# The first norm's scales as diagonal matrices, matmuls on ones ahead of it, and another order of the first loads

## The chip, the cores and the metric

The kernel runs on one core of one Trainium2 chip. The metric is device microseconds of one execution; the kernel before was run three times (median 1280.13 us). A core has five engines with an in-order queue each: TensorE (PE, its weight loads shown apart as PEld), VectorE (DVE), ScalarE (ACT), GpSimd (POOL) and SyncE (SP), which here issues every DMA. Engines wait for each other by semaphores; a waiting instruction holds up all that stands behind it on its engine.

## The reference

One decoder layer on 1024 tokens of 1024 channels, in float32:

```python
h = rms_norm(x, norm_pre_mix)          # x * rsqrt(mean(x*x) + eps) * g, row by row
p = h @ w_in                           # 1024 x 2720: conv columns, r, k, v, and low-rank wd, ad, gd
...                                    # token shift, RWKV-7 recurrence over 8 heads of 64,
decay = f(tanh(wd) @ decay_up)         # the two low-rank products that the change speaks of
a = sigmoid(iclr_a0 + ad @ iclr_up)
g = sigmoid(gd) @ gate_up
...                                    # causal convolution (31 taps), layer norm, silu
x = x + rms_norm(concat(rwkv, conv) @ w_out, norm_post_mix)
f = conv_ffn(rms_norm(x, norm_pre_ffn))   # 1024 -> 2 x 2816 -> 1024, 3-tap convolution, gelu gate
out = x + rms_norm(f, norm_post_ffn)
```

The change touches only the first norm, the projection's beginning and the loading of the low-rank weights.

## The kernel before

**Precision.** PE multiplies float32 operands at full speed only in a rounded form. Every product is therefore made of three matmuls: both operands are split into a high part (a rounded copy) and a low part (the difference), and hi x hi, hi x lo and lo x hi are summed. For a weight, `weight` (L164) loads it into `wr` (three buffers), ACT casts it to `wh` and POOL subtracts to get `wl` (both at L162, two buffers each). In the first half of the tokens SP also stores each `wl` to DRAM (`lows`, L183), for the second half to read it back (L179); a `wl` buffer can be written again only when PE has read it and its store has landed.

**Order.** The kernel is written with a tile framework. Work belongs to streams with priorities (`PRIO`), `first` ahead of all others; the framework's scheduler merges the streams by priority and its own estimate of times into one fixed order for each engine. `tc.issue_after(i)` keeps what stands under it behind instruction `i` in that order.

**The beginning.** The tokens are taken in halves of 512. For the first half, four row tiles `l` (128 tokens by 1024 channels, as two pieces of 256 KB each) are loaded (`load_rows`, L287) and normed in two pairs (`norm_rows`, L293). For row tiles 0 and 2 ACT sums the squares (L308); for 1 and 3 DVE does it by statistics (L301). DVE forms mean + eps (L156), POOL takes the reciprocal root (L157), ACT scales one piece of the row (L311) and DVE the other (L312). Then `channels` (L258) turns the pair: PE transposes sixteen 128x128 blocks against an identity (L150) into PSUM banks `pe` and `pb`, ACT writes the high part of `h`, scaled by the channel's gain (L277), and DVE the low part (L279). `h` has eight tiles of 128 channels, each with a high and a low part.

Then PE projects. The first weight pair belongs to k0; it is used in two halves of 256 columns, so that the first pair of row tiles suffices to begin (`project` with `halves`, 48 matmuls of 256 columns). The first and second weight of this text are the two halves of k0's first block of 128 outputs, the third and fourth those of its second block (24 matmuls of 512 columns on 128 outputs each), the fifth and sixth are `w_wa`, the columns `wd` and `ad` (64 outputs). After these come k1, r0, r1, and the chunked recurrence of the first quarter.

**Beside it.** The second half's rows (`mixr`, `ck`, `co`) are loaded and normed early, behind the last `h` of the first half. The low-rank weights (`lora`, `lw`) are loaded in `setup_mixer` (L233 to L240): three loads, two casts on ACT, two subtractions on POOL.

The FFN's first norm (`norm_ffn`, L874) does not scale its rows: it multiplies the identity by the root (a diagonal matrix), and PE multiplies the row by that diagonal, which transposes and scales in one matmul. `channels` takes these matrices as `diags`.

## Time and profile before

| | before |
|---|---|
| runs | 1280.13 us median (1280.02 to 1281.09) |
| profiled execution | 1282.25 us, its span 1280.5 us |
| granted TensorE clock, mean | 0.988 |
| busy share of the span | PE 96%, PEld 78%, DVE 70%, ACT 57%, POOL 39% |
| DMA | 185.70 MB, mean 145 GB/s |

A row of a timeline reads: start, duration, engine, source line, operation, output tile <- input tiles, shape, number of instructions merged, and in brackets how long the engine had been idle before it and what ended that. A row of a group reads: instructions merged, then busy us and mean ns of one, then idle us before them and what ended most of it. `SPq` rows are issues of DMAs by SP, not the transfers.

### The profile page before, as it was taken

Reading aid. Unit: us, or ns where it says so; the run is one execution under the profiler, and the core shown is the slowest. Engines: PE = TensorE matmul, PEld = TensorE weight load, DVE = VectorE, ACT = ScalarE, POOL = GpSimd, SP = SyncE. Lnnn points to the kernel's source line nnn. Section 1 sums busy time; section 2 is a strip of 40 time slices with the busy share of each in tenths; the row PEclk is TensorE's granted clock in tenths of the full one; section 3 lists DMA queues with packets and bytes.
Section 4 is the critical chain, followed back from the end, with each engine's and each line's share of the span. In section 5 each row is a group of like instructions: output and inputs, shape, how many; then the busy total and the mean of one; then the engine's idle time right before and its main releaser. Section 6 shows DMA issues by size and latency. Waiting matters only on the chain.

```text
span 1280.5 us, 23025 instructions
## 1 busy us (share of the span) xinstructions
PE 1231.8 (96%) x8460; PEld 993.7 (78%) x8460; DVE 892.2 (70%) x1540; ACT 731.3 (57%) x1518; POOL 495.6 (39%) x438
## 2 busy tenths in 40 slices
PE   6989989999999989999999999999999999999997
PEld 5767767787778867788789878787778888888885
DVE  5286998997679989996621275655366678479568
ACT  6563564655844865656743277777455566444451
POOL 4343320011113332344455269897688860000001
PEclk9999999999999999999999999999999999999999
DMA  7544442343342461222345498887423245335523
GB/s 241 171 137 138 118 127 76 107 133 116 109 131 89 133 192 44 84 79 80 108 137 159 133 335 304 287 310 238 157 67 82 71 159 190 91 114 187 162 73 132
DMA packets 105505, 185.70 MB, mean 145 GB/s; under 512 B 15184, under 2 KB 21712, under 8 KB 105392
## 3 DMA queue, kind: packets, MB, share of 16 engines
q1 hardware_dynamic: 105392, 184.23, 45.5%
q8 instruction: 67, 1.10, 0.4%
q14 instruction: 46, 0.38, 0.1%
HBM read 141.58 MB, written 42.60 MB: 144 GB/s over the span
## 4 chain that ended last, share of the span: by engine, by line
PE 58%; DVE 8%; issue 2%; POOL 2%; DMA 2%; ACT 2%; SPq 0%; POOLq 0%; DVEq 0%; ACTq 0%
PE pb L135 27%; PE pe L135 13%; PE xs L135 12%; PE Y L135 2%; PE pc L135 2%; DVE pc L416 2%; DVE nrow L1116 1%; POOL wl L162 1%; DVE x L1100 1%; PE pc L150 1%; DMA pt<-mixd 1%; DMA m<-mixd 1%; POOL b L1056 1%; PE pe L150 0%; DVE m L162 0%
## 5 line engine op out<-in xcount | busy, mean ns | idle before, releaser
L162 POOL TENSOR_TENSOR wl<-wr,wh 128x512 fp32r<-128x512 f32 (+1 forms) x181 | 237.5, 1314 | 251.0 <-ACT wh L162 219.8
L162 ACT CAST wh<-wr 128x512 fp32r<-128x512 f32 (+1 forms) x220 | 135.4, 616 | 174.4 <-issue 46.1
L135 PE MATMUL pb<-h,wh 128*128 128x512 f32 (+3 forms) x720 | 228.8, 397 | 3.2 <-ACT wh L162 1.6
L135 PE MATMUL pb<-f,wh 128*128 128x512 f32 x696 | 221.9, 399 | 2.5 <-ACT wh L162 1.5
L416 DVE SCALAR_TENSOR_TENSOR pc<-c,params,pc 128x512 f32<-128x512 f32 x232 | 174.3, 751 | 8.7 <-ACT pc L413 4.7
L135 PEld LDWEIGHTS pb<-h,wh 128*128 128x128 f32 (+2 forms) x720 | 131.2, 188 | 36.0 <-ACT wh L162 3.7
L135 PEld LDWEIGHTS pb<-f,wh 128*128 128x128 f32 x696 | 130.9, 190 | 32.4 <-ACT wh L162 2.8
L135 PE MATMUL pb<-h,wl 128*128 128x512 f32 (+3 forms) x360 | 146.1, 406 | 2.1 <-POOL wl L162 2.0
L135 PE MATMUL pb<-f,wl 128*128 128x512 f32 x348 | 139.0, 400 | 0.9 <-POOL wl L162 0.9
L157 POOL TENSOR_TENSOR ss<-var,mhalf 128x1 f32<-128x1 f32 x16 | 11.0, 692 | 226.9 <-DVE ss L1097 202.8
L1056 POOL TENSOR_TENSOR b<-b,b 128x512 f32<-128x512 f32 x66 | 86.9, 1319 | 2.6 <-DMA b<-ffn_down 1.0
L135 PE MATMUL pe<-f,wh 128*128 128x512 f32 x272 | 85.4, 395 | 0.1
L135 PEld LDWEIGHTS pb<-h,wl 128*128 128x128 f32 (+2 forms) x360 | 67.3, 187 | 20.1 <-POOL wl L162 4.1
L135 PEld LDWEIGHTS pb<-f,wl 128*128 128x128 f32 x348 | 66.3, 190 | 16.7 <-POOL wl L162 2.0
L135 PE MATMUL xs<-f,wh 128*128 128x512 f32 x200 | 62.7, 395 | 0.4 <-DVE act L953 0.4
L135 PEld LDWEIGHTS pe<-f,wh 128*128 128x128 f32 x272 | 51.0, 188 | 11.7 <-ACT wh L162 0.3
L899 DVE SCALAR_TENSOR_TENSOR pt<-pb,params,pt 128x511 f32<-128x511 f32 (+1 forms) x48 | 35.7, 744 | 31.6 <-ACT ecarry L892 31.1
L162 POOL TENSOR_TENSOR wl<-b,wh 128x512 fp32r<-128x512 f32 x36 | 47.0, 1305 | 22.4 <-ACT wh L162 20.7
L135 PE MATMUL pe<-f,wl 128*128 128x512 f32 x136 | 53.8, 396 | 0.7 <-POOL wl L162 0.7
L706 POOL TENSOR_TENSOR XG<-r,GE 64x256 f32<-64x256 f32 x30 | 20.4, 683 | 87.1 <-DVE r L725 82.3
L178 ACT CAST wh<-wr 128x512 fp32r<-128x512 f32 (+2 forms) x44 | 26.5, 604 | 43.5 <-PE pb L135 31.2
L162 ACT CAST wh<-b 128x512 fp32r<-128x512 f32 x36 | 22.2, 617 | 47.4 <-PE pb L135 19.2
(428 smaller groups left out, 2896.8 us busy)
## 6 DMA issues: line engine op xcount, KB each, us to landing
wr<-ffn_up SPq DMA_DIRECT2D x117, 256.0 KB, 2.8
wr<-w_in SPq DMA_DIRECT2D x80, 256.0 KB, 3.0
b<-ffn_down SPq DMA_DIRECT2D x44, 256.0 KB, 4.4
sums<-b SPq DMA_DIRECT2D x44, 256.0 KB, 3.9
wr<-sums SPq DMA_DIRECT2D x44, 256.0 KB, 2.7
lows<-wl SPq DMA_DIRECT2D x40, 256.0 KB, 3.3
wl<-lows SPq DMA_DIRECT2D x40, 256.0 KB, 2.6
b<-ffn_up SPq DMA_DIRECT2D x40, 256.0 KB, 2.7
```

The costliest lines, as they stand in the source:

```text
L135: return self.nc.tensor.matmul(out, lhsT, rhs, start=start, stop=stop, skip_group_check=skip)
L150: self.nc.tensor.transpose(out, in_, self.con("ident")[:n, :n])
L157: self.nc.gpsimd.tensor_tensor(out, v[:, :n], self.mhalf[:, :n], ALU.pow)
L162: return self.nc.scalar.copy(hi, src), eng.tensor_tensor(lo, src, hi.bitcast(F32), ALU.subtract)
L178: self.nc.scalar.copy(hi, raw)
L416: nc.vector.scalar_tensor_tensor(out, c[:, j:j + HALF], w(j), acc, ALU.mult, ALU.add)
L706: nc.gpsimd.tensor_tensor(x[64:128], R[64:128, gs], w.GE[64:128, c, gs].unsqueeze(2).broadcast_to([64, 4, CH]), ALU.mult)
L899: nc.vector.scalar_tensor_tensor(acc[:, o:], ps[:, :HALF - o], w(j), acc[:, o:], ALU.mult, ALU.add)
L1056: sub = lambda o, x, y, op=ALU.subtract: self.nc.gpsimd.tensor_tensor(o, x, y, op)
L1100: nc.vector.scalar_tensor_tensor(x, f[c], s[:, 1:2], x, ALU.mult, ALU.add)
L1116: nc.vector.tensor_tensor(out, a, b, op)
```

## The change

1. **Diagonals.** `norm_rows` takes `dg`; for the first half's rows it no longer scales, but writes a 128x128 diagonal for each row tile into one `pt` tile. `channels` then multiplies by these. The second pair uses the PSUM banks `pc`, `xs` (two) and `Y`, which have no other use yet, instead of `pe` and `pb`.
2. **Ones.** POOL fills a tile with ones, and PE multiplies it by itself seven times (`WARM`) into bank `pc`, before anything else. The result is not used.
3. **Order of the first loads.** Now: identity, row tiles 0 and 1, parameters, the first two weights, row tiles 2 and 3, the other constants.
4. **Low-rank weights later.** Their three loads and four operations move from `setup_mixer` to `lora_in`, behind the load and the subtraction of the sixth weight in the scheduler's order, with `t2` tiles for the raw form.
5. **The second half's rows** are loaded behind the issue of the third weight's load.

```diff
+WARM = 7
...
             if self.loaded:
                 raw = self.loaded.pop(0)
+            else:
+                raw = (self.f2p.tile(...) if held is self.hp else self.wp.tile(shape, F32, tag="wr", bufs=3, ...))
+                self.load = self.nc.sync.dma_start(raw, src)
+                self.loads.append(self.load)
...
+        with self.stream("first"):
+            warm = self.tl("co", [P, 512])
+            nc.gpsimd.memset(warm, 1.0)
+            ps = self.bank("pc")
+            for _ in range(WARM):
+                self.mm(ps, warm[:, :P], warm)
+            nc.sync.dma_start(self.const[:, :P], a["consts"][:, :P])
+            two = [self.tl("l8", [P, 2, D]) for _ in range(2)]
+            self.rows = [(two[t // 2][:, t % 2, :512], two[t // 2][:, t % 2, 512:]) for t in range(4)]
+            self.load_rows(0, self.rows[:2])
+            nc.sync.dma_start(self.params, a["params"])
+            for j in range(2):
+                raw = self.wp.tile([P, 4, P], F32, tag="wr", bufs=3, name=self.nm("wr"))
+                self.load = nc.sync.dma_start(raw, a["w_in"][4, j])
+                self.loaded.append(raw)
+            self.load_rows(0, self.rows[2:], 2)
+            nc.sync.dma_start(self.const[:, P:], a["consts"][:, P:])
...
+    def lora_in(self):
+        nc, a = self.nc, self.a
+        for e in range(2):
+            raw = self.tl("t2", [P, D_RWKV])
+            nc.sync.dma_start(raw, a["lora"][:, e])
+            nc.scalar.copy(self.lw[:, e], raw[0:96])
+            low = self.lw[64:96, e]
+            nc.gpsimd.tensor_tensor(low, raw[64:96], low.bitcast(F32), ALU.subtract)
+        nc.sync.dma_start(self.lora, a["lora"][:G_LORA, 2])
...
             self.rstd(ss[:, 3:4], ss[:, 2:3], 1.0 if t % 2 else 1.0 / D, RMS_EPS)
-            nc.scalar.activation(row[0], row[0], AF.Copy, scale=ss[:, 3:4])
-            nc.vector.tensor_scalar(row[1], row[1], ss[:, 3:4], None, ALU.mult)
+            if dg is not None:
+                nc.vector.tensor_scalar(dg[:, t], self.con("ident"), ss[:, 3:4], None, ALU.mult)
+            else:
+                nc.scalar.activation(row[0], row[0], AF.Copy, scale=ss[:, 3:4])
+                nc.vector.tensor_scalar(row[1], row[1], ss[:, 3:4], None, ALU.mult)
...
+            dg = self.tl("pt", [P, 4, P])
             for b in range(2):
-                two = rows[2 * b:2 * b + 2]
-                self.norm_rows(two)
-                self.channels(two, "pre_mix", hs, slice(b * QUARTER, (b + 1) * QUARTER), ("pe", "pb", "pb"))
+                two = self.rows[2 * b:2 * b + 2]
+                self.norm_rows(two, dg[:, 2 * b:2 * b + 2])
+                self.channels(two, "pre_mix", hs, slice(b * QUARTER, (b + 1) * QUARTER),
+                              ("pc", *self.xs, self.Y) if b else ("pb", "pe"), [dg[:, 2 * b + t] for t in range(2)])
...
-        project(0, hs, "k0 w k1 r0 r1")
+        project(0, hs, "k0 w")
+        behind = self.loads[0], self.load, self.low
+        project(0, hs, "k1 r0 r1")
...
-            self.load_rows(1, rows)
+            with tc.issue_after(behind[0].ins):
+                self.load_rows(1, rows)
+            with tc.issue_after(behind[1].ins), tc.issue_after(behind[2].ins):
+                self.lora_in()
```

The scheduler lays all engines anew from this. Three places of its order follow. The first is POOL at the beginning, where `ss<-var` is the reciprocal root of a row tile, `wl<-wr` the low part of a weight and `lw` that of a low-rank weight. Before:

```order
L157 TENSOR_TENSOR ss_220<-var_226,mhalf 128x1
L240 TENSOR_TENSOR lw<-wr_106,lw 32x512
L240 TENSOR_TENSOR lw<-wr_110,lw 32x512
L162 TENSOR_TENSOR wl_274<-wr_271,wh_273 128x512
L162 TENSOR_TENSOR wl_281<-wr_278,wh_280 128x512
L157 TENSOR_TENSOR ss_689<-var_695,mhalf 128x1
L157 TENSOR_TENSOR ss_700<-var_706,mhalf 128x1
L157 TENSOR_TENSOR ss_711<-var_717,mhalf 128x1
L157 TENSOR_TENSOR ss_722<-var_728,mhalf 128x1
L162 TENSOR_TENSOR wl_340<-wr_337,wh_339 128x512
```

and with the change, from the first half's first root on:

```order
L161 TENSOR_TENSOR ss_157<-var_163,mhalf 128x1
L166 TENSOR_TENSOR wl_271<-wr_114,wh_270 128x512
L161 TENSOR_TENSOR ss_167<-var_173,mhalf 128x1
L166 TENSOR_TENSOR wl_276<-wr_116,wh_275 128x512
L161 TENSOR_TENSOR ss_213<-var_219,mhalf 128x1
L161 TENSOR_TENSOR ss_223<-var_229,mhalf 128x1
L161 TENSOR_TENSOR ss_693<-var_699,mhalf 128x1
L166 TENSOR_TENSOR wl_335<-wr_332,wh_334 128x512
L161 TENSOR_TENSOR ss_704<-var_710,mhalf 128x1
L166 TENSOR_TENSOR wl_354<-wr_351,wh_353 128x512
```

The first two weights' low parts now stand among the first half's roots, and the third's and fourth's (`wl_335`, `wl_354`) among the second half's, where before all of these came ahead of the third (`wl_340`).

The second place is SP from the store of the first low part on. Before:

```order
L183 DMA lows<-wl_274 128x512
L170 DMA wr_379<-w_wa 128x256
L183 DMA lows<-wl_281 128x512
L170 DMA wr_398<-w_wa 128x256
L183 DMA lows<-wl_340 128x512
L170 DMA wr_423<-w_in 128x512
L183 DMA lows<-wl_359 128x512
```

and with the change:

```order
L191 DMA lows<-wl_271 128x512
L191 DMA lows<-wl_276 128x512
L825 DMA po_4713<-post_mix 128x256
L177 DMA wr_393<-w_wa 128x256
L277 DMA t_114_684<-lora 128x512
L277 DMA t_115_688<-lora 128x512
L281 DMA lora<-lora 96x512
L177 DMA wr_418<-w_in 128x512
L191 DMA lows<-wl_335 128x512
L191 DMA lows<-wl_354 128x512
```

The store of the third low part (`wl_340`, now `wl_335`) stood right behind the load of the sixth weight; now three low-rank loads and a seventh weight's load stand between.

The third place is PE at about half of the mixer's first part, where a projection (`pb<-h`) and the recurrence's last step (`xs<-r`, `Y<-r`) meet. Before, nine matmuls of that projection stand ahead of the recurrence, the last of them and the first two of the recurrence being:

```order
L135 MATMUL pb_1890<-h_139,wh_1893 128x512
L135 MATMUL pb_1890<-h_140,wh_1893 128x512
L135 MATMUL pb_1890<-h_139,wl_1894 128x512
L135 MATMUL xs_97<-r_267,ck_1108 64x64
L135 MATMUL Y<-r_267,ca_1041 64x64
```

and with the change:

```order
L139 MATMUL pb_1894<-h_140,wh_1897 128x512
L139 MATMUL pb_1894<-h_141,wh_1897 128x512
L139 MATMUL xs_94<-r_266,ck_1112 64x64
L139 MATMUL Y<-r_266,ca_1045 64x64
```

Two of the nine are left ahead, and seven come behind. From here to the end of the mixer such small shifts run through all engines' orders; behind the mixer the orders are the same.

## The prediction

> **What bounds the kernel now.** I read the page first: which engine is full, and in which part of the span it is not.

> ```profile
> span 1280.5 us, 23025 instructions
> PE 1231.8 (96%) x8460; PEld 993.7 (78%) x8460; DVE 892.2 (70%) x1540; ACT 731.3 (57%) x1518; POOL 495.6 (39%) x438
> ```

> TensorE (PE) is busy for 96% of the span, so a gain has to come out of 48.7 us of PE idle time or out of slow matmuls. The table of windows says where the idle time lies (the columns are window, length, busy time and count for PE, PEld, DVE, ACT, POOL, then granted clock, DMA share, GB/s).

> ```profile
> 0.00:20.00 20.00, 8.48 (x32) 5.97 (x32) 11.04 (x36) 13.56 (x31) 6.82 (x14) 1.00 0.91 305
> 20.00:60.00 40.00, 39.27 (x184) 31.20 (x185) 14.70 (x39) 22.73 (x45) 18.16 (x17) 1.00 0.54 165
> 60.00:640.00 580.00, 556.80 (x5358) 444.23 (x5357) 487.55 (x871) 352.56 (x731) 166.05 (x166) 0.98 0.37 111
> ```

> The change works on the first of them: 11.5 us idle, nearly a quarter of the total. From 20 to 60 us PE misses only 0.7 us, so a lead won at 20 us is kept as far as every feeder of PE keeps pace, and a lead that a feeder does not follow turns into a stall. So I looked next at the timeline of PE over the first projection (k0's first block, 48 matmuls of 256 columns) and the start of the two behind it.

> ```profile
> 8.46 0.48 PE L150 MATMUL pe<-const,l 128*128 128x128 f32 x1 [8.46 <-ACT l L311]
> 20.37 0.77 PE L135 MATMUL pb<-h,wh 128*128 128x256 f32 x2 [0.48 <-DVE h L279]
> 20.93 0.41 PE L135 MATMUL pb<-h,wl 128*128 128x256 f32 x1
> 21.14 0.63 PE L135 MATMUL pb<-h,wh 128*128 128x256 f32 x2
> 27.96 0.28 PE L135 MATMUL pb<-h,wl 128*128 128x256 f32 x1
> 28.08 0.63 PE L135 MATMUL pb<-h,wh 128*128 128x512 f32 x2
> 28.84 0.50 PE L135 MATMUL pb<-h,wl 128*128 128x512 f32 x1
> 34.42 0.39 PE L135 MATMUL pb<-h,wl 128*64 128x512 f32 x1
> ```

> At 21 us matmuls of one size start 0.21 us apart (20.93 to 21.14); at 28 us, 0.12 apart (27.96 to 28.08). PE begins this projection at half rate, although the clock column of the first window reads 1.00. That block ends at 28.08; the third weight's low part is first read at 28.84, the fifth weight's (`w_wa`) at 34.42. These two times are my gauges.

> **The change on PE alone.** A scaled row was two passes (L311 0.72 us, L312 0.48); a diagonal is one small one, and the sixteen transposes of each pair of row tiles become sixteen true matmuls.

> ```profile
> L311 ACT ACTIVATE l<-l,ss 128x512 f32<-128x512 f32 x4 | 2.9, 723 | 1.9 <-POOL ss L157 1.9
> L312 DVE TENSOR_SCALAR l<-l,ss 128x512 f32<-128x512 f32 x4 | 1.9, 476 | 0.0
> 488.92 0.28 DVE L874 TENSOR_SCALAR kk<-const,sf 128x128 f32<-128x128 f32 x1
> 496.17 1.05 PE L135 MATMUL pb<-kk,row 128*128 128x128 f32 x8
> 39.48 1.02 PE L135 MATMUL pe<-kk,const 128*128 128x512 f32 x2
> ```

> The FFN's first norm already does it so: 0.28 us a diagonal, and 8 records in 1.05 us are 4 matmuls of two records, about 0.22 us each at full rate, twice that at half. ACT is rid of 2.9 us, DVE of 1.9 - 4 x 0.28 = 0.8. Seven matmuls on ones are fourteen records; two last some 0.9 us at full rate (1.02 with the last one's tail), so the seven take 6 us, or 12 at half rate, and begin near 1.3 us. They are hidden behind the row loads either way: the second diagonal is not ready before 11.9 us (below). Without that cover they would cost up to 12 us.

> The last diagonal stands at 15.0 to 15.5 us (next part). Fourteen diagonal matmuls behind it (3.1 us) and 48 x 0.12 = 5.8 us of k0 end at 23.9 to 24.4: **PE alone would be 3.7 to 4.2 us ahead** of 28.08.

> Whether the ones keep the rate up until then, the rows leave open: PE has little between the first diagonal (an estimate: 9.4, behind five small operations on the parameters) and the second. If all sixteen to thirty-two diagonal matmuls ran at half rate, k0 would end near 27. I price this at nothing, since the next part is as late; without that cover it is 2.5 us.

> **What PE then waits for: the third weight's low part.** Here the order of the queues counts, and each is in order.

> ```profile
> l<-x SPq DMA_DIRECT2D x8, 256.0 KB, 5.4
> params<-params SPq DMA_DIRECT2D x1, 185.0 KB, 6.5
> 8.00:11.00 3.00, 1.32 (x4) 0.58 (x4) 2.57 (x8) 2.51 (x6) 0.55 (x1) 1.00 1.05 373
> 7.96 0.69 DVE L301 BATCH_NORM_STATS2 bs<-l 128x6 f32<-128x512 f32 x1 [1.01 <-DMA l<-x]
> 9.67 0.55 POOL L157 TENSOR_TENSOR ss<-var,mhalf 128x1 f32<-128x1 f32 x1 [2.02 <-DVE var L156]
> 9.95 0.69 DVE L301 BATCH_NORM_STATS2 bs<-l 128x6 f32<-128x512 f32 x1 [0.36 <-DMA l<-x]
> 9.27 0.63 ACT L308 ACTIVATE pt<-l 128x512 f32<-128x512 f32 x1
> L162 ACT CAST wh<-wr 128x512 fp32r<-128x512 f32 (+1 forms) x220 | 135.4, 616 | 174.4 <-issue 46.1
> ```

> Loads: SP now issues the parameters (185 KB) and the first two weights (512 KB) ahead of row tiles 2 and 3. The seventh of the eight row pieces landed at 9.95, so the eighth, at 373 GB/s, near 10.65. It now has 697 KB more ahead of it: 1.9 us at that rate, 2.3 at the 305 GB/s of the first window. It lands at **12.5 to 13.0**.

> Norm: from a piece's arrival to its root is 9.67 + 0.55 - 7.96 = 2.26 us, and 0.28 for the diagonal: 15.0 to 15.5. On POOL the second root now stands behind the first weight's subtraction. That weight ends 1465 KB of loads (four row pieces, 185, 256), where before the sixth row piece ended 1536 KB and was squared at 9.27: there by 9.2, cast 0.6, subtraction 1.3, root 0.55, diagonal 0.28: 11.9. The second weight's subtraction follows, through by 13, before the last root's input at 14.

> ```profile
> 17.78 1.66 DVE L279 SCALAR_TENSOR_TENSOR h<-pe,params,h 128x256 fp32r<-128x256 f32 x4 [0.36 <-ACT h L277]
> 20.92 0.87 DVE L279 SCALAR_TENSOR_TENSOR h<-pe,params,h 128x256 fp32r<-128x256 f32 x2
> 21.70 1.28 DVE L301 BATCH_NORM_STATS2 bs<-mixr 128x6 f32<-128x512 f32 x2
> 22.90 1.27 DVE L301 BATCH_NORM_STATS2 bs<-co 128x6 f32<-128x512 f32 x2
> 24.52 2.59 POOL L157 TENSOR_TENSOR ss<-var,mhalf 128x1 f32<-128x1 f32 x4 [0.67 <-DVE ss L309]
> 27.47 1.31 POOL L162 TENSOR_TENSOR wl<-wr,wh 128x512 fp32r<-128x512 f32 x1 [0.36 <-ACT wh L162]
> ```

> All sixteen low parts of h now stand on DVE behind the last diagonal: 16 x 1.66/4 = 6.6 us, so 21.6 to 22.1. Before they ended at 20.92 + 0.87 = 21.8: DVE has won nothing. Behind them come the second half's statistics, whose first root ended at 24.52 + 0.65, 3.3 us after 21.8: now 24.9 to 25.4. And POOL now holds the third weight's subtraction behind that root, where before all four roots were long done: + 1.3 us, 26.2 to 26.7, against 28.8. **2.3 us are left of PE's lead at the first gauge**; PE waits near 25 us for about 1.5 to 2.

> **And then for the fifth: a store that SP holds back.**

> ```profile
> 28.81 0.33 SPq L170 DMA_DIRECT2D wr<-w_wa  x1
> 29.19 0.42 SPq L183 DMA_DIRECT2D lows<-wl  x1
> 33.14 0.74 POOL L162 TENSOR_TENSOR wl<-wr,wh 128x256 fp32r<-128x256 f32 x1 [2.63 <-DMA lows<-wl]
> ```

> `wl` has two buffers, so the fifth low part may be written only when the third has been stored to DRAM: 29.19 to 33.14, 3.95 us, and POOL sat idle 2.63 for it. Before, that store stood right behind the second `w_wa` load. Now SP has three low-rank loads (704 KB by their shapes) and the next `w_in` load between, and that last one needs the fourth weight's buffer, which POOL frees after one more root and subtraction: 0.65 + 1.3 = 1.95 us after 26.2 to 26.7. Its own issue takes 0.4 more: store at 28.6 to 29.1, back by 32.5 to 33.0, subtraction (0.74) done by 33.3 to 33.8, against a read at 34.42: **0.6 to 1.1 us of lead at the second gauge.** Bounds: the 704 KB are 1.9 us of transfer at 373 GB/s; if all of them are still queued, the lead turns into a loss of 1 us; if the store lands 0.8 us faster, it is 1.8. I take 0.6, the low end, since by 28.6 most of the 704 KB, issued from 26.5 on, have moved, but not all. Preparing the low-rank weights itself (two casts, two subtractions of 1.25 us) falls where POOL waits for the store, and its user comes after 55 us: nothing.

> Sum: 1282.25 us for the profiled execution - 0.6 = 1281.6; that execution stands 2.1 above the median of the runs, so against 1280.13 I say **1279.5**.

> **Rivals.** (A) *The lead holds.* If the store is back in time, 2.3 us stay; if the two weights do not delay the rows either, PE's 4 us. Middle: 3.1, so 1277.0. For it: 20 to 60 us leaves PE no other wait. Against: the 2.63 us wait on that very store.

> (B) *New gaps bring the half rate back, and the kernel gets slower.* The place is the two waits made above, near 25 and 32 us.

> ```profile
> 388.32 1.62 PE L150 MATMUL pe<-const,l 128*128 128x128 f32 x8 [2.15 <-DVE mixr L760]
> 389.00:392.00 3.00, 3.00 (x14) 2.78 (x13) 3.00 (x8) 2.87 (x6) 0.00 (x0) 0.50 0.20 76
> 392.00:393.00 1.00, 1.00 (x5) 0.53 (x4) 1.00 (x4) 1.00 (x3) 0.00 (x0) 0.93 0.00 0
> ```

> After a gap of 2.15 us the granted clock was 0.50 for 3.4 us: 1.7 us lost. One such stretch gives 1281.2, two or a third in the middle 1282.9; it decides from the second on, as PE is full behind it. [...]

> (C) *The middle is re-laid.* The scheduler's order differs on all engines from about 165 us to the end of the mixer, and is the same from there on.

> ```profile
> 180.00:190.00 10.00, 6.92 (x120) 5.12 (x120) 9.87 (x17) 9.23 (x20) 1.44 (x3) 0.87 0.29 100
> 190.00:200.00 10.00, 9.27 (x34) 7.17 (x34) 9.89 (x16) 3.73 (x6) 0.00 (x0) 0.62 0.00 0
> ```

> Here PE loses 1.3 + 3.8 us to the clock and 3.8 idle. Seven matmuls of a projection now come behind the recurrence and could fill it: up to 3.5 us, 1276.5. Against: DVE is full there and sets the pace.

> (D) *The ones do not do what they are for* (half rate at 16 us): by the price above the time stays the forecast's, so it is no case of its own.

> **Chances.** Forecast 0.40 (its own range 1278.3 to 1280.8), A 0.22, B one stretch 0.10, B two 0.12, C 0.16. Differences under 0.2% (2.6 us) can hardly be told from none. A and C lie mostly below 1277.6: 0.35 faster. B with two lies above 1282.7: 0.13 slower. The rest, 0.52, within. The range for eight times in ten runs from 1276.0, inside A's and C's better ends, to 1282.4, short of B's second stretch.

> **What would show it.** Right: the third weight's subtraction on POOL behind a root, ending near 26.5; PE gaps near 25 and 32 us; POOL idle on the store of `wl` before the fifth; first read of the fifth weight's low part within 1 us of 34.4. The start: 256-column matmuls 0.12 apart from the first if the ones work, 0.21 if not. Wrong: a fifth low part read before 32.5 (A), a clock of 0.50 between 25 and 40 us (B), or a lead that changes by more than 2 us between 160 and 640 us (C).

## The result and the profile after

| | before | changed |
|---|---|---|
| runs taken together | 1281.63 us median of 6 (1280.02 to 1286.07) | 1289.60 us median of 6 (1286.40 to 1292.94) |
| ratio | 1 | 1.0060, 95% interval 1.0037 to 1.0082 |
| profiled execution | 1282.25 us | 1286.4 us, its span 1284.6 us |

The kernel became slower by 0.6%, 8.0 us between the medians. I had forecast 1279.5 with a range up to 1282.4. A second set of six runs of the changed kernel gave 1289.61 (1.0066, 1.0044 to 1.0088). The runs of this text come in six sets; the kernel before was run again in each, and its medians lie between 1281.5 and 1282.8 us. A difference between medians of two sets can be off by as much; the ratios compare within a set.

The page after, its first lines, and the table of windows with the cuts of before (the last window is longer by the difference of the spans):

```profile
span 1284.6 us, 23107 instructions
PE 1241.2 (97%) x8506; PEld 996.9 (78%) x8506; DVE 894.8 (70%) x1540; ACT 729.0 (57%) x1515; POOL 494.9 (39%) x439
```

```profile
0.00:20.00 20.00, 17.31 (x91) 12.39 (x92) 11.67 (x37) 12.08 (x29) 5.97 (x14) 1.00 0.91 318
20.00:60.00 40.00, 36.64 (x173) 28.15 (x172) 15.97 (x38) 22.13 (x44) 19.26 (x18) 1.00 0.52 158
60.00:640.00 580.00, 558.75 (x5358) 444.76 (x5356) 488.50 (x866) 350.73 (x728) 163.19 (x165) 0.98 0.38 111
```

PE is busy for 8.8 us more in the first 20 us (8.5 of it are the ones), for 2.6 us less from 20 to 60, for 2.0 us more from 60 to 640. The share of busy time rose, and the kernel is slower: busy time alone says nothing here.

PE's timeline at the places that the prediction timed, in the changed kernel:

```profile
1.32 8.48 PE L139 MATMUL pc<-co 128*128 128x512 f32 x14 [1.32 <-POOL mhalf L209]
12.06 0.94 PE L139 MATMUL pb<-pt,l 128*128 128x128 f32 x6 [1.37 <-DVE pt L338]
18.39 0.48 PE L139 MATMUL pb<-h,wh 128*128 128x256 f32 x2
18.71 0.28 PE L139 MATMUL pb<-h,wl 128*128 128x256 f32 x1
18.83 0.40 PE L139 MATMUL pb<-h,wh 128*128 128x256 f32 x2
24.22 0.63 PE L139 MATMUL pb<-h,wh 128*128 128x512 f32 x2
26.09 0.50 PE L139 MATMUL pb<-h,wl 128*128 128x512 f32 x1 [1.24 <-POOL wl L166]
33.53 0.45 PE L139 MATMUL pb<-h,wl 128*64 128x512 f32 x1 [1.69 <-POOL wl L166]
```

In this execution the start went as forecast. The ones end at 9.8 us (one matmul on them, float32 as it is and two records, takes 0.86 us at the full clock of 5.8 to 9.6 us; one on the rounded parts, with the same 512 columns, 0.23 at 26.4 to 26.9); matmuls of 256 columns are 0.12 us apart from the first (18.71 to 18.83); k0's first block ends at 24.22 (forecast 23.9 to 24.4, before 28.08). The third low part is read at 26.09 (26.2 to 26.7, before 28.84), the fifth at 33.53 (33.3 to 33.8, before 34.42). What holds the fifth back is what the prediction named. SP's issues and POOL's work there:

```profile
26.44 0.91 SPq L277 DMA_DIRECT2D t<-lora  x2
27.39 0.43 SPq L281 DMA_DIRECT2D lora<-lora  x1
28.41 0.90 SPq L191 DMA_DIRECT2D lows<-wl  x2
```

```profile
24.78 1.26 POOL L166 TENSOR_TENSOR wl<-wr,wh 128x512 fp32r<-128x512 f32 x1
32.76 1.42 POOL L166 TENSOR_TENSOR wl<-wr,wh 128x256 fp32r<-128x256 f32 x2 [3.52 <-DMA lows<-wl]
```

The third low part is done at 26.04, its store is issued at 28.41, behind the low-rank loads, and POOL is idle for 3.52 us until it has landed. So at 34 us the changed kernel was 0.9 us ahead, and at the end 4 us behind, one execution against one. It lost 5 us in a part of the program whose instructions the change does not touch.

To see where, I took the same matmuls of PE in every trace (those at 38, 145, 268, 505, 700 and 1270 us in the kernel before; the first is one of the last of `w_wa`) and the time from one to the next. The number in brackets is an estimate of what granted clock of 0.50 cost there: half of the time at 0.50, since matmuls of 512 columns start 0.43 us apart at 0.50 and 0.23 at 1.00 (the changed kernel's first trace, 74.3 to 79.8 us).

| trace | at | 38-145 | 145-268 | 268-505 | 505-700 | 700-1270 |
|---|---|---|---|---|---|---|
| before | 38.1 | 106.9 (0) | 123.0 (5.1) | 237.0 (5.1) | 195.0 (3.4) | 570.0 |
| changed, first trace | 37.3 | 108.5 (1.7) | 124.5 (6.8) | 238.1 (5.1) | 194.1 (0) | 571.8 |
| changed, second trace | 39.7 | 107.8 (1.7) | 124.6 (6.8) | 238.9 (3.4) | 195.7 (1.7) | 570.2 |
| new start, old middle | 38.4 | 107.5 (1.7) | 122.8 (5.1) | 237.9 (5.1) | 191.9 (0) | 572.9 |
| old start, new middle | 39.8 | 107.7 (0) | 125.0 (6.8) | 241.1 (5.1) | 194.1 (0) | 571.1 |
| first piece new | 38.5 | 107.8 (0) | 124.7 (6.8) | 235.9 (1.7) | 191.9 (0) | 572.8 |
| middle piece new | 37.8 | 107.0 (1.7) | 124.0 (6.8) | 241.6 (5.1) | 191.6 (0) | 573.3 |
| first and middle piece new | 37.9 | 108.3 (1.7) | 124.5 (6.8) | 238.4 (5.1) | 191.6 (0) | 570.0 |
| first piece and end new | 39.8 | 107.9 (0) | 124.8 (6.8) | 235.8 (1.7) | 196.1 (1.7) | 573.3 |
| eight ones | 36.3 | 107.0 (0) | 129.3 (6.8) | 243.3 (3.4) | 192.6 (1.7) | 572.2 |
| ten ones | 36.0 | 106.8 (0) | 123.7 (6.8) | 246.7 (5.1) | 190.5 (1.7) | 573.1 |
| both stores first, nine ones | 34.3 | 107.1 (1.7) | 122.8 (5.1) | 239.3 (6.8) | 193.4 (1.7) | 571.1 |

In the rows of eight and ten ones the order differs at the cuts themselves, so there only the sum from 145 to 700 us can be compared (565.2 and 560.9; before 555.0). One trace is one execution, and executions of one kernel scatter by some 3 us to either side of their median (the six of the changed kernel run from 1286.4 to 1292.9), so the table says where to look and the medians below decide.

### The profile page after: what moved, and what is told of

It reads as the page before. It is cut to its first block, busy times and chain, and to the rows that moved or that the text cites. A ratio compares the mean times of both kernels' runs of the same rounds, so it can differ in the third digit from the quotient of the medians.

```text
span 1284.6 us, 23107 instructions
## 1 busy us (share of the span) xinstructions
PE 1241.2 (97%) x8506; PEld 996.9 (78%) x8506; DVE 894.8 (70%) x1540; ACT 729.0 (57%) x1515; POOL 494.9 (39%) x439
## 4 chain that ended last, share of the span: by engine, by line
PE 69%; DVE 15%; ACT 5%; issue 4%; DMA 4%; POOL 3%; SPq 0%; POOLq 0%; DVEq 0%; ACTq 0%
PE pb L139 35%; PE pe L139 15%; PE xs L139 13%; DVE pc L445 4%; PE Y L139 2%; PE pc L139 2%; POOL wl L166 2%; DMA lows<-wl 1%; DVE nrow L1145 1%; PE pe L154 1%; DVE x L1129 1%; ACT wh L166 1%; DMA pt<-mixd 1%; DVE sub L620 1%; PE pc L154 1%
## 5 line engine op out<-in xcount | busy, mean ns | idle before, releaser
L139 PEld LDWEIGHTS pb<-h,wl 128*128 128x128 f32 (+2 forms) x360 | 67.0, 186 | 24.9 <-POOL wl L166 8.2
L186 ACT CAST wh<-wr 128x512 fp32r<-128x512 f32 (+2 forms) x44 | 26.4, 604 | 40.2 <-PE pb L139 26.4
## 6 DMA issues: line engine op xcount, KB each, us to landing
wr<-ffn_up SPq DMA_DIRECT2D x117, 256.0 KB, 2.9
wr<-w_in SPq DMA_DIRECT2D x80, 256.0 KB, 3.0
b<-ffn_down SPq DMA_DIRECT2D x44, 256.0 KB, 4.5
sums<-b SPq DMA_DIRECT2D x44, 256.0 KB, 3.7
wr<-sums SPq DMA_DIRECT2D x44, 256.0 KB, 2.7
lows<-wl SPq DMA_DIRECT2D x40, 256.0 KB, 3.4
wl<-lows SPq DMA_DIRECT2D x40, 256.0 KB, 2.7
b<-ffn_up SPq DMA_DIRECT2D x40, 256.0 KB, 2.7
```

The source lines that it names most:

```text
L139: return self.nc.tensor.matmul(out, lhsT, rhs, start=start, stop=stop, skip_group_check=skip)
L186: self.nc.scalar.copy(hi, raw)
```

## Start against middle

The diff touches the start, but the scheduler laid the whole mixer anew. I separated the two: the instructions of the mixer from its first quarter to its end (6310, made in the same sequence in both kernels) were chained on every engine, without a semaphore, in the order in which the other kernel has them.

```diff
+    def pin(self, made):
+        for eng, place in orders_of_the_other_kernel.items():
+            mine = [i for i in made if str(i.engine) == "EngineType." + eng]
+            for p, q in zip(place, place[1:]):
+                self.tc.add_manual_dep(mine[q], mine[p].name,
+                    mybir.DependencyInfo(mybir.DependencyClass.NoSync, mybir.DependencyReason.DATA))
...
+        mark = len(nc.cur_bb.bb.instructions)
         weave(quarter(0))
         project(0, hs, "v0 v1 g")
...
+        self.pin(nc.cur_bb.bb.instructions[mark:])
         return h0
```

**The changed kernel again.**

> The changed kernel as it is, once more, as the yardstick for the three runs beside it and for a second trace. Both theories: 1.004 to 1.008 of the kernel before. Theory M (the middle): the order of the mixer's middle, which the scheduler laid anew, costs some 4 us, and the start itself gains about 1. Theory S (the start): the new first 60 us cost it, by what they hold (diagonals, ones, loads, low-rank weights), later and out of sight of the first two gauges.

Measured: 1289.61 us (6 runs), 1.0066 (1.0044 to 1.0088).

**New start, old middle.**

> The changed kernel's start, with the instructions of the mixer from the first quarter to its end held on every engine in the order of the kernel before. Theory M: the start's lead of 0.9 us at the fifth weight stays, 0.9990 to 1.0003 of the kernel before. Theory S: as slow as the changed kernel, 1.004 to 1.008. If parts do not add (an order suits only the start it was laid for): slower than the changed kernel.

Measured: 1283.99 us (12 runs), 1.0014 (0.9998 to 1.0029): 5.6 us below the changed kernel, and not below the kernel before.

**Old start, new middle.**

> The reverse: the start of the kernel before, with the mixer's middle in the changed kernel's order. Theory M: 1.004 to 1.008 of the kernel before, some 1 us above the changed kernel. Theory S: 0.999 to 1.001, as the kernel before. If parts do not add: slower than either.

Measured: 1288.35 us (8 runs), 1.0046 (1.0030 to 1.0062).

The middle's order costs 5.6 us with the new start and 6.3 with the old one. The new start is no gain: it is slower by 1.9 us with the old middle and by 1.3 with the new one, both hardly to be told from zero. Theory M holds for the middle; its gain of the start does not show in the time.

## Which part of the middle

In the traces with the new order two places repeat. The first is the half-clock stretch near 187 us, in the changed kernel and in its twin with the old middle (windows cut where the clock changes):

```profile
183.28:186.69 3.41, 1.58 (x50) 1.13 (x48) 3.41 (x6) 3.34 (x8) 0.00 (x0) 1.00 0.31 100
186.69:200.34 13.65, 12.33 (x55) 9.36 (x56) 13.62 (x22) 8.50 (x16) 0.21 (x1) 0.50 0.08 19
200.34:203.75 3.41, 3.41 (x21) 2.50 (x21) 3.09 (x5) 0.62 (x1) 0.00 (x0) 1.00 0.27 59
```

```profile
187.85:198.09 10.24, 8.21 (x30) 6.16 (x29) 10.21 (x16) 5.70 (x10) 0.21 (x1) 0.50 0.00 0
198.09:201.50 3.41, 3.41 (x17) 2.54 (x15) 3.27 (x6) 0.62 (x1) 0.00 (x0) 1.00 0.14 25
```

The stretch is 3.4 us longer. The seven matmuls that I expected to fill PE's idle time are not in it: they run ahead of it, at full clock (between the recurrence's last step and this stretch the projection has 22 matmuls, until 183.2 us; in the twin it has 15, until 182.3). Behind them PE waits for the recurrence's next step, in the changed kernel and in the twin:

```profile
185.20 0.21 PE L139 MATMUL pe<-l 32*32 32x32 f32 x1 [1.64 <-ACT l L676]
```

```profile
183.43 0.21 PE L303 MATMUL pe<-l 32*32 32x32 f32 x1 [0.79 <-ACT l L840]
```

On ACT this `l` stands behind an operation that waits for DVE's `kk`, done at 183.25 us in the changed kernel and at 180.96 in the twin. Counted from the matmul of 145 us, the step comes 2.0 us later than in the twin. DVE is full in both stretches (13.62 of 13.65 us, 10.21 of 10.24), and in its new order `kk` comes later; so the fuller PE did not help. The second place is the mixer's end, PE and ACT of the changed kernel's second trace:

```profile
644.04 0.73 PE L139 MATMUL pb<-f,wh 128*128 128x512 f32 x2 [1.30 <-ACT wh L166]
645.63 0.50 PE L139 MATMUL pb<-f,wl 128*128 128x512 f32 x1 [0.86 <-POOL wl L166]
```

```profile
641.30 2.16 ACT L166 CAST l<-co 128x512 fp32r<-128x512 f32 x4
643.37 0.61 ACT L166 CAST wh<-wr 128x512 fp32r<-128x512 f32 x1
```

Four casts of the convolution stand ahead of a weight's cast, and PE waits. The old order has one such wait of PE (2.1 us in all from 505 to 700), the new one two (3.5 us). I cut the middle in three, at about 268 and 505 us, where both orders have issued the same instructions, and combined the pieces.

**First piece new.**

> The changed start; the mixer's middle in the changed kernel's order up to about 268 us of the span, in the order of before from there on. Theory M in two places: of the 5.6 us between the changed kernel (1289.6) and its twin with the old middle (1284.0), some 2.1 sit between 145 and 200 us (a half-clock stretch 13.65 us long instead of 10.24, in all three traces with the new order) and some 2.2 at 630 to 645 us. Then this one is 1.5 to 2.5 us above the twin, 1285.5 to 1286.5. Rival (the sum of many small shifts, or an order that only works as a whole): 1284 or anything up to 1289.6, and no longer stretch at 187 us.

Measured: 1283.87 us (12 runs), 1.0012 (1.0000 to 1.0023). The longer stretch is there (187.91 to 201.56 us), 145 to 268 us takes 1.9 us more, and the time is that of the twin. In its trace the next piece, in the old order, took 235.9 us, at the lower end of what it takes in ten traces with the old middle (235.3 to 240.9), and nothing of the 1.9 us is left at 505.

**First and middle piece new, old end.**

> The changed kernel with the order of before only from about 505 us to the end of the mixer. Theory M in two places: the waits of PE for a weight's cast behind ACT's four casts of the convolution (2.1 us near 644 us) go, 1.5 to 2.5 us below the changed kernel: 1287 to 1288. Rival: 1289.6, PE finds another wait there or the clock takes it.

Measured: 1290.62 us (7 runs), 1.0057 (1.0035 to 1.0079). The waits at the end are gone from the trace (191.6 instead of 194 to 196 us), and the time did not fall (this trace is of the fastest of the seven runs, 1282.96). Both places that I had picked from the traces decide nothing by themselves.

**Middle piece new.**

> The changed start; the mixer in the order of before, but in the changed kernel's order from about 268 to 505 us. Two readings of the runs so far contradict each other. From the medians: the first piece costs 0 (1283.9 against 1284.0), the end 0 or less (1290.6 against 1289.6), so this middle piece alone costs all 5.6 to 6.7 us: 1289.5 to 1291. From the aligned traces: the first piece 2.7, this piece 1.0, the end 2.0 us or more: 1285.

Measured: 1288.17 us (9 runs), 1.0049 (1.0032 to 1.0067).

**First piece and end new, old middle piece.**

> The complement: the changed kernel with the order of before from about 268 to 505 us only. From the medians: the cost goes, 1283 to 1285. From the aligned traces: 1288 to 1289. If neither this nor its complement agrees with either, the pieces do not add, and a cost depends on how late PE comes to a piece.

Measured: 1287.98 us (6 runs), 1.0046 (1.0030 to 1.0061).

The two readings named in the expectations are both off: this middle piece is below the one's 1289.5 and above the other's 1285, its complement agrees with the traces.

Over the twin (1284.0) that is, in us: first piece -0.1, middle piece 4.2, first and end 4.0, first and middle 6.6, all three 5.6. Each of these has an interval of some 2.5 to 3.5 us to either side (an estimate from the two intervals that it combines). Pieces of 1, 4 and 1.5 us come within 1.6 us of all five; so the middle piece probably carries the larger part (it adds 4.2 us alone, 6.7 behind the new first piece, 1.6 between two new ones), and no place alone carries all. How the cost divides is not shown beyond that, and which instructions cost it the single traces do not show; that stays open. That PE's delay in one piece is given back in the next where another engine sets the pace is likely by the first run of these, and not shown.

**Other layouts.** The scheduler's layout follows from its own estimates, so a trifle in the start is enough to get another. I changed only the number of ones, with nothing held.

```diff
-WARM = 7
+WARM = 4
```

> The changed kernel with four matmuls on ones instead of seven and nothing held in place. With four, the scheduler lays the mixer's middle as in the kernel before, row by row; so this shows the old middle without any pinning. If the middle's order costs the 5.6 us: like the twin with the old middle, 1284.0, plus what three ones are worth (without any it was 1287.0, so 0 to 3 us): 1284 to 1287. If the pinning itself had done something: 1289 to 1292.

Measured: 1286.16 us (12 runs), 1.0034 (1.0020 to 1.0048): between 1284.0 and the 1286.95 without ones (below), and below the changed kernel's 1289.6. So the old middle is the better one also when the scheduler itself lays it, and the twin's gain does not come from the holding. The 2.2 us above the twin have no single cause here: the scheduler also laid the start anew (the fourth diagonal, for one, comes on DVE at 17.9 us instead of 15.4).

> The changed kernel with eight matmuls on ones and nothing held in place: one more matmul on PE's first 10 us, and a third order of the middle, further from that of before (on DVE over 1100 of 1542 rows stand elsewhere) than the changed kernel's. If the time depends on which order the scheduler happens to lay, and that of before is a good one: 1286 to 1292. If an order that differs more costs more: over 1292. If only the changed kernel's order is bad: 1283 to 1285.

Measured: 1297.40 us (6 runs), 1.0127 (1.0101 to 1.0154).

> The same with ten ones and a fourth order of the middle. As for eight; beside this, ten end near 13 us, past the second diagonal (12.4), and may push the first block back by up to 1 us, which the store of the third low part hides.

Measured: 1289.93 us (6 runs), 1.0076 (1.0059 to 1.0093).

One more matmul on ones, hidden behind the row loads, goes with 7.8 us more (1297.40 against 1289.61). The start is not what loses them: with eight and ten ones the scheduler also moved the third low part's store one place ahead on SP, and the fifth low part is read at 32.6 and 32.2 us, earlier than with seven. PE's waits from 145 to 505 us with eight ones (waiting tile, who ended it, us in total, times, longest):

```profile
PE xs L139 <- ACT XG L733: 2.7, 2, 1.4
PE pe L139 <- ACT l L676: 2.1, 3, 1.6
PE xs L139 <- ACT r L744: 2.0, 3, 1.0
PE pe L139 <- ACT pt L510: 2.0, 1, 2.0
```

These are steps of the recurrence. In the twin with the old middle the first of them is 0.4 us, and the longest wait of all 2.2. Against the twin with the old middle the three other layouts are slower by 5.6 (seven ones), 13.4 (eight) and 5.9 us (ten). That a layout further from the old one costs more, which the expectation for eight ones named for a time over 1292, agrees with these three (between the twin and eight ones most rows have moved), and three layouts do not show it. Of the four layouts measured, that of the kernel before is the best, and what threatens a change in this kernel is to lose it.

## Parts of the start

**Without the ones**, all else in the same order on every engine.

```diff
-WARM = 7
+WARM = 0
```

> As the changed start with the old middle, but without the seven matmuls on ones, all else on every engine in the same order. By the prediction (the store of the third low part sets the pace, PE's rate does not): PE runs the first block at 0.21 us per 256-column matmul and ends it near 28 us, the fifth weight is read near 34.2, and the time is 0 to 1 us above its twin with ones. Rival: the ones are what the start is worth; without them the diagonals and the block run at half rate and the time is 3 us or more above the twin.

Measured: 1286.95 us (9 runs), 1.0040 (1.0022 to 1.0058), 3.0 us above the twin. The rival's number came, but only in part by its way. The first pair's diagonals ran at half rate (until 17.5 us, see the last section), but the 256-column matmuls did not: they are 0.12 us apart, and the first block ends at 27.0 us, not near 28 as expected. The half rate also reaches the next queue, which the prediction had left out: DVE's low parts of `h` wait for the diagonals' products, the second half's statistics begin at 23.15 us instead of 21.83, the third low part's subtraction at 26.60 instead of 25.23, and the fifth low part is read at 35.61 instead of 34.68. In the traces the run without ones is 0.9 us behind at 38 us (39.3 against 38.4) and 0.3 at 145. So the runs say that the ones are worth about 3 us (with an interval of some 3 to either side), and the traces show under 1; where the rest goes is open.

**Scaled rows instead of diagonals.**

```diff
-                self.norm_rows(two, dg[:, 2 * b:2 * b + 2])
+                self.norm_rows(two)
                 self.channels(two, "pre_mix", hs, slice(b * QUARTER, (b + 1) * QUARTER),
-                              ("pc", *self.xs, self.Y) if b else ("pb", "pe"), [dg[:, 2 * b + t] for t in range(2)])
+                              ("pc", *self.xs, self.Y) if b else ("pb", "pe"))
```

> The changed start with the old middle, but the first norm's rows are scaled as before (ACT and DVE) and transposed against the identity; ones, loads and low-rank weights as in the change. By the prediction the diagonals shorten the way from the last root to its row tile by about 0.4 us and rid ACT of 2.9 and DVE of 0.8 us, all of it hidden behind the store of the third low part: 0 to 1 us above its twin with diagonals (1284.0). Rival: the diagonals carry the start: 2 us or more above.

Measured: 1282.74 us (12 runs), 1.0008 (0.9996 to 1.0021), 1.3 us below the twin with diagonals, whose interval it overlaps. No gain of the diagonals shows. But not all else is the same: the start was not held, and in it the third low part's store stands one place further ahead on SP, directly behind the low-rank loads (issued at 28.32 us); the fifth low part is read at 33.41, in the twin at 34.68. By the next section a store's place alone can be worth as much (2.8 us), so the run does not show what the diagonals are worth with the stores alike.

## The stores on SP

The twin with the old middle has the prediction's two waits (PE: 1.24 us before the third low part, 2.35 before the fifth). In these runs rows of SP, POOL and ACT at the beginning were moved and the start held, each run with the moves of those before it; the middle is the old one.

**The third low part's store first.**

```diff
 wr<-w_wa
+lows<-wl_335
 t<-lora
 t<-lora
 lora<-lora
 wr<-w_in
-lows<-wl_335
 lows<-wl_354
```

> The changed start with the old middle, and one move on SP: the store of the third weight's low part stands directly behind the load of the sixth weight, ahead of the three low-rank loads and the seventh weight's load. By the prediction's second gauge (the store held back on SP sets the fifth weight): the store is issued near 27 instead of 28.9 us and nothing is ahead of it in transfer, so the fifth low part is read near 32 instead of 34.7 us, PE's gap there falls under 0.5 us, and the time falls by 1.5 to 2.5 us, to about 1282, 0.999 to 1.001 of the kernel before. Rival: the start's lead is lost further on whatever the store does: 1284.

Measured: 1281.20 us (12 runs), 0.9992 (0.9981 to 1.0002), 2.8 us below the twin. PE no longer waits for the fifth low part; now the sixth is late, behind the fourth's store, which comes behind the low-rank loads. SP's issues, and PE's wait:

```profile
26.77 0.43 SPq L369 DMA_DIRECT2D lows<-wl  x1
27.25 0.92 SPq L455 DMA_DIRECT2D t<-lora  x2
28.21 0.43 SPq L459 DMA_DIRECT2D lora<-lora  x1
29.15 0.43 SPq L369 DMA_DIRECT2D lows<-wl  x1
```

```profile
35.65 0.45 PE L317 MATMUL pb<-h,wl 128*64 128x512 f32 x1 [0.68 <-POOL wl L344]
```

**And the low parts ahead of the roots on POOL.**

```diff
+wl_335<-wr_332,wh_334
 ss_693<-var_699,mhalf
-wl_335<-wr_332,wh_334
+wl_354<-wr_351,wh_353
 ss_704<-var_710,mhalf
-wl_354<-wr_351,wh_353
```

> As the run with the store first, and also on POOL the third weight's subtraction ahead of the second half's first root and the fourth's ahead of its second, on ACT the fifth weight's cast ahead of the second and third scaled row. By the prediction (POOL's order sets the first gauge): the third low part is read near 24.9 instead of 26.1 to 26.6 us, the fifth near 30.5, both gaps of PE go, and the time is 3 to 4.5 us below the twin with the old middle: 1279.5 to 1281, 0.998 to 0.9995 of the kernel before, so below both kernels. Rival: the lead is lost before 145 us to the weights' loads and stores, or to the half-clock stretch near 75 us: 1282 to 1284.

On ACT the fifth weight's cast moved ahead too, by two scaled rows. Measured: 1282.55 us (12 runs), 0.9989 (0.9975 to 1.0004): the 1279.5 to 1281 that I expected did not come, and against the run before (0.9992) no gain shows. In its trace, of the slowest of the twelve runs, the wait before the third low part is gone, but the clock fell to 0.50 at 13 us (six records of the second diagonal last 1.65 us; 0.94 in the run before), behind PE's idle time of 2.16 us between the first and the second diagonal, and PE came to the matmul of 38 us at 37.4 instead of 36.6. What the order on POOL is worth by itself stays open.

**And the low-rank loads behind the fourth low part's store.**

```diff
 lows<-wl_335
-t<-lora
-t<-lora
-lora<-lora
 wr<-w_in
 lows<-wl_354
+t<-lora
+t<-lora
+lora<-lora
 wr<-w_in
```

> As the run with store and low part first, and the low-rank loads behind the store of the fourth low part too (in that run the sixth low part waited for that store until 35.6 us, issued at 30.3 behind 704 KB of loads), the low-rank casts on ACT behind the sixth weight's cast. By the theory that stores held up in SP's queue set the pace of the start: sixth weight read without a wait, the projection about 1 us earlier at 38 us than with the first store alone (36.6), and 1279.5 to 1280.5 in all. Rival: the lead is again eaten before 60 us by the next stores: 1281 to 1282.5.

On ACT the two low-rank casts moved back behind the sixth weight's cast. Measured: 1279.82 us (12 runs), 0.9985 (0.9975 to 0.9996). The matmul of 38.1 us comes at 34.6, 2.0 us before the run with the first store alone.

**And nine ones**, held like the rest.

> As the run before this, with nine matmuls on ones instead of seven. They end near 11.9 instead of 9.8 us, and the idle time of PE between the first diagonal's matmuls and the second diagonal (1.8 to 2.2 us, near 11 us) goes, and with it the chance of a half-clock stretch at 13 us (seen in one of six traces with ones, 2.3 us). Theory: 0 to 1 us below the run with seven, and no half clock between 6 and 30 us. Rival: the first diagonal's matmuls come 2 us later and with them the rows of h: 0.5 to 1.5 us above.

Measured: 1280.23 us (12 runs), 0.9980 (0.9969 to 0.9992). Not to be told from seven; the idle time and the half clock at 13 us are gone from its trace and from the next.

> The version with both stores first, nine ones and the old middle once more, for a second set of runs and a second trace. If its 0.998 was no luck of twelve runs: 0.997 to 0.999 again, with the sixth weight read near 30 us without a wait before it. If it was: 0.999 to 1.0005.

Measured: 1279.90 us (12 runs), 0.9976 (0.9962 to 0.9991). PE at the two gauges in this trace, and its windows:

```profile
24.71 0.63 PE L317 MATMUL pb<-h,wh 128*128 128x512 f32 x2
25.45 0.50 PE L317 MATMUL pb<-h,wl 128*128 128x512 f32 x1
30.55 0.63 PE L317 MATMUL pb<-h,wh 128*64 128x512 f32 x2
31.02 0.39 PE L317 MATMUL pb<-h,wl 128*64 128x512 f32 x1
```

```profile
0.00:20.00 20.00, 18.69 (x91) 12.76 (x92) 11.10 (x36) 11.65 (x28) 5.96 (x14) 1.00 0.89 316
20.00:60.00 40.00, 39.89 (x192) 31.24 (x190) 16.45 (x40) 25.74 (x47) 19.87 (x18) 1.00 0.58 172
```

No wait is left at either gauge: the fifth low part is read at 31.02 (before 34.42), and PE misses 0.1 us from 20 to 60. The whole lead of 3.4 us is there, and most of it reaches the end: 0.998 of the kernel before in both sets, some 10 us below the changed kernel. This version is faster than both, by 0.2% and 0.8%.

## Why the prediction was wrong

**The step that failed is the price of the re-laid middle**: nothing in the sum, and in rival (C) a gain only. (C) had a chance of 0.16: "Seven matmuls of a projection now come behind the recurrence and could fill it: up to 3.5 us, 1276.5". I priced one place, 180 to 200 us; the seven matmuls ran ahead of it, and there DVE's new order made PE wait longer (1.64 us instead of 0.79). "DVE is full there and sets the pace" stood in the text as a reason against the gain; that the pace itself could get worse I did not ask. The rest of the middle, which the order shows to shift everywhere from 165 us to the mixer's end, I gave no price at all. What the runs showed in its place is a loss of 5.6 to 6.3 us. Yet the windows of before have a bound for it:

```profile
145.00:268.00 123.00, 119.12 (x1263) 91.81 (x1262) 113.35 (x196) 68.39 (x139) 20.04 (x26) 0.96 0.36 110
268.00:505.00 237.00, 224.54 (x2258) 186.38 (x2257) 200.95 (x393) 152.49 (x335) 54.72 (x60) 0.98 0.39 120
505.00:700.00 195.00, 192.81 (x1609) 161.06 (x1608) 126.14 (x190) 109.74 (x229) 91.91 (x74) 0.98 0.37 107
```

PE is idle for 18.5 us here and loses 13.7 to half clock (by the estimate of the table above). Where 32 us of loss depend on an order, an order laid anew can be worth several us either way, and towards the loss if the old one is good.

**The chain of the first 34 us was right in its mechanism, and one of its terms was too small.** The first trace is within 0.2 us of each range. The runs on the stores show that the queues named held the lead: the third low part's store alone is worth 2.8 us (1284.0 to 1281.2), and with the fourth's, POOL's subtractions and ACT's casts moved as well it is about 4 us (1284.0 to 1279.9), much like the 3.7 to 4.2 that PE has alone. The term that was too small is the store. In seven traces of the same start it took 4.35 to 5.0 us from its issue to the subtraction that waits for it, against 3.95 before, and the fifth low part was read between 33.5 and 34.8 us, in the middle one at 34.4, where the kernel before has 34.42. I had put 704 KB of loads ahead of the store and still calculated with 3.95; the bound of a loss of 1 us stood in the text. The forecast's 0.6 us is within that scatter (the only other trace of the old start reads the fifth at 36.05), and that the first trace agreed so well is partly luck. By the medians the start gains nothing.

**Rival (B), the half clock behind a new gap**, happens, but in some executions only: in the second trace of the changed kernel the wait of the fifth low part was followed by one stretch, as priced (1.7 us). From 35.16 us on, matmuls start 0.43 us apart, before the wait 0.23. PE's timeline there:

```profile
34.40 0.44 PE L139 MATMUL pb<-h,wl 128*64 128x512 f32 x1 [1.86 <-POOL wl L166]
34.68 0.68 PE L139 MATMUL pb<-h,wh 128*64 128x512 f32 x2
35.16 0.63 PE L139 MATMUL pb<-h,wl 128*64 128x512 f32 x1
35.59 0.63 PE L139 MATMUL pb<-h,wh 128*64 128x512 f32 x1
```

It came in two of the seven traces with this start and this wait. **(D)**, the ones failing, did not happen: the 256-column matmuls are 0.12 us apart from the first. Its price, nothing, was wrong too: without the ones the runs are 3.0 us slower, and the fifth low part comes 0.9 us later, since PE's half rate delays the next queue instead of hiding behind it. **(A)** needed what the change did not do; the last version does it.

The numbers together: 1279.5 was a forecast against a median of three runs, 1280.13, which is 1281.6 in six. Against that it says 1281.0; the start came 2.5 us worse than its 0.6 (of which the runs can tell little from zero), the middle 5.6: 1289.1, measured 1289.6.

## What to carry to other kernels

Where a scheduler lays the program, a change has two effects, what it does and how everything behind it is laid. Compare the orders, and where they differ away from the change, hold the old order there before judging the change: here the layout cost 5.6 us and hid a start that gains 2 to 3 (0.9985 to 0.9976 of the kernel before) once two stores stand ahead of three loads and the work on POOL and ACT is ordered alike. A store that frees a buffer belongs ahead of any load that nobody waits for on the same queue; here the third low part's store alone, moved so, was worth 2.8 us.

## What the hardware did that I had not expected

```profile
71.30:74.71 3.41, 1.93 (x7) 1.32 (x8) 3.00 (x3) 3.41 (x8) 3.33 (x3) 1.00 0.13 13
74.71:78.13 3.42, 3.42 (x16) 2.50 (x15) 3.35 (x7) 1.09 (x3) 1.35 (x2) 1.00 0.81 207
```

```profile
72.68:76.09 3.41, 1.61 (x6) 1.03 (x7) 2.90 (x4) 3.39 (x9) 3.14 (x3) 1.00 0.00 1
76.09:79.50 3.41, 3.41 (x10) 2.53 (x8) 3.34 (x7) 1.41 (x4) 0.76 (x1) 0.50 0.75 198
```

In the first, the grid divides the gaps between two steps (PE busy 1.93 of 3.41 us) and the clock stays; in the second most of both falls into one step (1.61) and the next runs at half. Over the 19 traces, from 30 to 1265 us, steps at full clock were followed by half clock so often (of the 88 followed by half, 6 are in the trace of the kernel before and 5 in the changed kernel's first):

| PE busy in the step | followed by half | by full |
|---|---|---|
| under 45% | 37 | 1 |
| 45 to 55% | 21 | 7 |
| 55 to 65% | 13 | 20 |
| 65 to 80% | 13 | 208 |
| over 80% | 4 | 6410 |

So the same two gaps were followed by one step at half clock in one execution (1.7 us, half of 3.41, an estimate) and by none in another, and part of the scatter of one kernel goes with the clock: of 118 executions of the kernel before, between 1277.1 and 1287.7 us, the 38 with a mean granted clock of 0.990 or more took 1280.7 us on average, the 26 with 0.986 or less 1284.0. Of the steps of 65% and more that half clock followed, those near 184 and 417 us, and one of 99% at 508 us in the kernel before, hold matmuls of 64x64 or 32x32; the busy share may not be all that counts.

**The clock column can say 1.00 where nothing is recorded.** The records of the granted clock begin at 23.5 us in the kernel before, at 17.5 without the ones and at 5.8 in the changed kernel's first trace, and just there the spacing of equal matmuls halves (from 0.21 to 0.12 us at 23.5; on the ones from 0.85 to 0.43 at 5.7). Until then PE ran at half rate (256-column matmuls are 0.21 us apart also where 0.50 is recorded, at 390 us in the kernel before), and the windows show 1.00. This is the half rate that the prediction read from the spacing; with the ones it ended some 18 us earlier than in the kernel before, and 12 earlier than without them.

**A store took longer behind loads.** The third low part's store took 3.95 us from its issue in the kernel before, and 4.35 to 5.0 us in the seven traces of the changed start, where 704 KB of loads had been issued in the 2 us ahead of it. With that store ahead of these loads, it was the fourth's turn, behind them: 5.7 us (from 29.15 to the subtraction at 34.87), while the third's was over within 3.4.
